# Latent attention, row-maximum and projection matmuls issued ahead of a step's weighted sums, and output weights split one step behind their transfer

## The chip, the cores and the metric

The kernel runs on one core of a Trainium2 chip. The metric is the device time of the whole program in microseconds. The core has a matrix engine (PE, with weight loads shown apart as PEld), a vector engine (DVE), an activation engine (ACT), a general engine (POOL) and an engine that issues transfers (SP). Each takes its instructions strictly in the order in which the program holds them, and waits at the head of that order for what the instruction needs.

## The reference, cut to what matters

One decoder layer on 1024 tokens of width 1024: an adaLN-modulated norm, one input projection, two groups of heads (sparse attention and latent attention), a gate, one output projection. The change lies in the latent attention and in the loading of the output weights:

```python
def mla_block(args):
    qn, qr, tc = args
    s = (jnp.einsum('bqhd,bkhd->bhqk', qn, k_nope)
         + jnp.einsum('bqhd,bkd->bhqk', qr, k_rot)).astype(jnp.float32) * scale
    p = masked_softmax(s, key_idx[None, :] <= tc[:, None])
    return jnp.einsum('bhqk,bkhd->bqhd', p.astype(v.dtype), v)
...
mixed = jnp.concatenate([o_nsa * jax.nn.silu(z_nsa), o_mla * jax.nn.silu(z_mla)], axis=-1)
x = x + gate[:, None, :] * (mixed @ w_out[l])
```

There are 8 latent heads. Products are kept near float32 by splitting each operand in a high and a low part and adding three matmuls.

## The kernel before, in words

The latent attention has 48 tasks, six for each head (heads 0 to 7, task = 6 x head + 0 to 5). A task is two tiles of 128 keys against up to 512 queries; its score tile is 896, 384, 1024, 1024, 896 and 384 columns wide for the six tasks of a head. The stage runs from about 533 us to 684 us. Step i of its loop (lines 1467 to 1482) does four things:

1. `scores_m(i)`: score matmuls into a PSUM tile `ms` (PE, L1301 to L1306); two exponentials of it on ACT, one in float32 (`lat`, L1314) and one in f16 (`mH`, L1315); their difference `mL` on DVE (L1316).
2. `weigh_m` of task i-3 (the flow is `MLA_LAG` = 3 tasks deep): the weighted sums `mo`, L937, 24 matmuls of 65 columns for a task of 1024 columns, 21 for 896, 9 for 384. After a head's half is complete, `merge_m` (L1324, L1325) scales it on DVE.
3. The entries of `plan` for step i. `max_m(h, ts)` computes raw scores of a later head on PE (`mm`, L1256) and takes their masked row maxima on DVE (`junkm`, `peak`, L1260), five turns in five steps; `peak_split` (DVE, `hl`, L1269 to L1272) and `max_rows` (a transposition `mn` on PE, L1276, a copy `mrow` on DVE, L1278, and two small transfers on SP, L1281) put the maxima in the rows of the queries that the scores of that head use. `kq_up` (L1180) projects keys or queries of a pair of heads and splits them on ACT (`kh`, `qh`, L1189) and DVE (`kl`, `ql`, L1190), with 6 or 12 matmuls at steps 13, 14, 25 and 26; `q_rot` and `v_up` do so at steps 5 to 7.
4. From step 27 on, one step of `load_wo`: a transfer of 256 KB of the output weights (`wor`, L1348, two buffers), its high part on ACT (`woh`, L1349) and its low part (`wol`, L1350) on DVE for odd pieces and on POOL for even ones. Eight pieces at steps 27 to 34. At steps 40 and 43 `mix_load` (L1358 to L1361) is called for the output stage: three transfers and a product on POOL.

`ms`, `mm`, `kq`, `vu`, `qr` and `mn` all take one of three PSUM buffers of 1024 columns. PE's order is the order of the program (`manual_schedule`); the other engines' orders are set by the scheduler of the framework, which hoists work that it takes to be ready, so the transfers of `mix_load` stand on SP just behind the first two of `wor`. The space of the `wor` buffers is that of the projection weights, so the first transfer waits for the last matmul of `kq_up` at step 26.

Of the kernel before, what the change touches and what calls it, by code (L numbers as in the profile page):

```python
# [94 lines left out]
def f32(ap):  # L95
    return ap.bitcast(F32)
# [11 lines left out]
def hybrid_block(ctx, tc, x, c, positions, ada_w, ada_b, norm_g, w_in, cmp_pos, cmp_k_w1, cmp_k_w2,  # L108
# [8 lines left out]
    def pool(stack, name, side="left"):  # L117
        return stack.enter_context(tc.tile_pool(name=name, bufs=1, side=side, reuse_waits="tile"))
# [693 lines left out]
    def drain(gen):  # L812
        for _ in gen:
            pass
# [336 lines left out]
    def slot(name):  # L1151
        return ps[0].tile([P, 1024], F32, tag="s", name=name, bufs=3)
# [136 lines left out]
    def scores_m(i):  # L1289
        h, hf, blks = tasks[i]  # L1290
        z = h % NSETS
        kh, kl, qh, ql = khs[z], kls[z], qhs[z], qls[z]
        pS = slot(f"ms{i}")
        spans, off = [], 0
        for j, c0 in blks:
            n = 512 - c0
            qs = slice(hf * 512 + c0, (hf + 1) * 512)
            ks = slice(j * P, (j + 1) * P)
            dst = pS[:, off:off + n]
            diag = j >= 4 * hf  # L1300
            nc.tensor.matmul(dst, kh[:98, ks], qh[:98, qs], start=n > 128, stop=False, skip_group_check=n < 257)  # L1301
            nc.tensor.matmul(dst, kh[:96, ks], ql[:96, qs], start=False, stop=False, skip_group_check=n < 257)  # L1302
            nc.tensor.matmul(dst, kl[:96, ks], qh[:96, qs], start=False, stop=not diag, skip_group_check=n < 257)  # L1303
            if diag and n != 256:
                two = n == 128
                nc.tensor.matmul(pS[:, off - 256 * two:off - 256 * two + 256 * (1 + two)].rearrange("p (b n) -> p b n", n=256)[:, :, :P]  # L1306
                                 if two else dst[:, :P], identr, dmr[:, None, :].to_broadcast([P, 2, P]) if two else dmr,
                                 start=False, stop=True, skip_group_check=two)
            spans.append((j, c0, off, n))
            off += n  # L1310
        Et = e_tile(i)
        ph = hlp.tile([P, 1024], F16, name=f"mH{i}", tag="H", bufs=HB)
        pl = hlp.tile([P, 1024], F16, name=f"mL{i}", tag="L", bufs=HB)
        nc.scalar.activation(Et[:, :off], pS[:, :off], AF.Exp, scale=SC_MLA)  # L1314
        nc.scalar.activation(ph[:, :off], pS[:, :off], AF.Exp, scale=SC_MLA)  # L1315
        nc.vector.tensor_tensor(pl[:, :off], Et[:, :off], ph[:, :off], op=ALU.subtract)  # L1316
        return spans, ph, pl
# [10 lines left out]
    def weigh_m(i, spans, ph, pl):  # L1328
        h, hf, _ = tasks[i]
        for j, c0, off, n in spans:  # L1330
            if j == 0:
                po_of[hf] = o_bank(f"mo{h}_{hf}", hf)
            for q in range(n // P):
                tq = c0 // P + q
                pv(po_of[hf], tq * 65, ph, pl, P, slice(off + q * P, off + (q + 1) * P), mp["v"][:, j, h],
                   j == 0 and q == 0, j == 4 * hf + 3)
        if spans[-1][0] == 4 * hf + 3:
            merge_m(h, hf)
# [4 lines left out]
    def load_wo(pl, hf):  # L1343
        for k in range(KD):
            woh[hf][k] = q_row((k % 4) + 8 * (k // 4)) if hf else pl.tile([P, 512], F32R, name=f"woh{hf}_{k}")
            wol[hf][k] = wol_place[k] if hf else pl.tile([P, 512], F32R, name=f"wol{hf}_{k}")
            wr = pl.tile([P, 512], F32, name="wor", tag="wor", bufs=2)
            nc.sync.dma_start(wr, w_out[k * P:(k + 1) * P, hf * 512:(hf + 1) * 512])  # L1348
            nc.scalar.activation(woh[hf][k], wr, AF.Copy)  # L1349
            (nc.vector if k % 2 else nc.gpsimd).tensor_tensor(wol[hf][k], wr, f32(woh[hf][k]), op=ALU.subtract)  # L1350
            yield

    mixs = {}

    def mix_load(t, pl):
        mix = mixs[t] = pl.tile([P, D], F32, name=f"mix{t}", tag="mix", bufs=2)
        zn = pl.tile([P, 512], F32, name=f"zn{t}", tag="zn", bufs=1)
        nc.sync.dma_start(mix[:, :512], mix_dram[t * P:(t + 1) * P, :])  # L1358
        nc.sync.dma_start(zn, z_dram[t * P:(t + 1) * P, :512])
        nc.sync.dma_start(mix[:, 512:], z_dram[t * P:(t + 1) * P, 512:])  # L1360
        nc.gpsimd.tensor_tensor(mix[:, :512], mix[:, :512], zn, op=ALU.mult)  # L1361
# [24 lines left out]
    def e_tile(i):  # L1386
        if i < LAG:
            return npool.tile([P, 1024], F32, name=f"mE{i}", tag="E", bufs=EB)
        if i < E_MIX:
            return mixm[1][:, 2 * (i % 2):2 * (i % 2) + 2].rearrange("p a n -> p (a n)")  # L1390
        return lat_flat[:, (i % 2) * 1024:(i % 2 + 1) * 1024]
# [59 lines left out]
    plan = {PLAN0[0]: [(kq_up, 1, 0)]}  # L1451
# [13 lines left out]
    with tc.manual_schedule(engines={mybir.EngineType.PE}):  # L1465
        wo_steps = iter(())
        for i in range(LAG, len(tasks)):
            if i in pre:
                for f, *args in pre[i]:
                    f(*args)  # L1470
            flow.append((i, *scores_m(i)))
            if len(flow) > MLA_LAG:
                weigh_m(*flow.pop(0))
            for f, *args in plan.pop(i, ()):
                f(*args)
            if i == MLA_WO:
                mr.close()
                wo0 = pool(att, "wo0", "right")
                wo_steps = load_wo(wo0, 0)
            next(wo_steps, None)  # L1480
            if i in MLA_MIX:
                mix_load(MLA_MIX.index(i), wo0)
        for f in flow:
            weigh_m(*f)
        drain(wo_steps)
# [5 lines left out]
    for n, tiles in enumerate((khs, qhs, kls, qls)):  # L1491
        wol_place += [tiles[1][:, :512], tiles[1][:, 512:]]
    drain(load_wo(op, 1))
    gf = lat_flat[:, 2048:3072]
    nc.sync.dma_start(gf, bass.AP(tensor=final_norm_g.tensor, offset=final_norm_g.offset, ap=[[0, P], [1, D]]))
# [100 lines left out]
```

## Time and profile before

| | us |
|---|---|
| median of 3 runs (lowest, highest) | 787.88 (786.41, 790.76) |
| the profiled execution, whole | 788.64 |
| its span, first to last instruction | 786.9 |
| mean granted clock of PE | 0.97 of full |
| PE busy in the span | 739.3 (94%) |
| DVE busy in the span | 583.6 (74%) |
| ACT busy in the span | 396.3 (50%) |

The profile is of one execution. [...]

### The profile page before, as it was taken

What the parts mean: (1) busy time and instruction counts of PE and PEld (TensorE: products, weight loads), DVE (VectorE), ACT (ScalarE), POOL (GpSimd) and SP (SyncE); (2) the same over time, 40 slices, a digit from 0 to 9 for tenths busy, and PEclk for the clock granted to TensorE, in tenths of its full rate; (3) what the DMA queues carried; (4) which work ended last, traced back from release to release, by engine and by line L of the source; (5) the groups of instructions that cost most, each with busy time, mean ns of one, the idle gap of its engine ahead of it and who ended that gap; (6) DMA issues with size and microseconds to landing.
All of it is one profiled execution on the core that took longest, in us unless ns stands there. A gap on an engine that the chain in (4) does not pass through costs nothing.

```text
span 786.9 us, 17257 instructions
## 1 busy us (share of the span) xinstructions
PE 739.3 (94%) x6464; PEld 653.9 (83%) x6464; DVE 583.6 (74%) x1549; ACT 396.3 (50%) x697; POOL 228.0 (29%) x287
## 2 busy tenths in 40 slices
PE   4999999999999999997899999999988989999996
PEld 3988998989999999995677887777877777888885
DVE  3688745587688788888898889987888878654433
ACT  5354534133122331217899977987556566632212
POOL 3334433154231143504443312110200040154322
PEclk9599999999999999999999999999999979999999
DMA  8961423242531121103311123013010140435431
GB/s 307 262 197 49 127 55 108 61 121 80 162 95 48 44 52 47 36 31 97 93 47 44 43 56 82 22 57 80 10 28 16 52 151 29 151 131 185 144 113 54
DMA packets 60513, 70.18 MB, mean 89 GB/s; under 512 B 5957, under 2 KB 46728, under 8 KB 60430
## 3 DMA queue, kind: packets, MB, share of 16 engines
q1 hardware_dynamic: 55646, 64.62, 27.8%
q10 hardware_dynamic: 4784, 4.47, 1.7%
q8 instruction: 51, 0.84, 0.4%
q14 instruction: 32, 0.26, 0.1%
HBM read 48.33 MB, written 11.53 MB: 76 GB/s over the span
## 4 chain that ended last, share of the span: by engine, by line
PE 76%; DVE 9%; issue 4%; ACT 4%; DMA 4%; POOL 2%; SPq 1%; POOLq 0%; DVEq 0%; ACTq 0%
PE pj L589 24%; PE out L1528 11%; PE o L937 5%; PE pm L841 4%; PE s L994 3%; PE s L995 3%; PE kcT L321 2%; PE mo L937 2%; PE hid L642 2%; PE kq L1180 2%; PE ms L1301 2%; DVE L L1010 2%; PE ms L1302 2%; PE ms L1303 2%; PE mm L1256 2%
## 5 line engine op out<-in xcount | busy, mean ns | idle before, releaser
L589 PE MATMUL pj<-whi,hh 128*128 128x288 f32 (+2 forms) x544 | 161.4, 297 | 0.0
L589 PE MATMUL pj<-wlo,hh 128*128 128x288 f32 (+2 forms) x544 | 158.6, 292 | 0.0
L589 PE MATMUL pj<-whi,hl 128*128 128x288 f32 (+2 forms) x544 | 157.6, 290 | 0.0
L589 PEld LDWEIGHTS pj<-wlo,hh 128*128 128x128 f32 x544 | 102.5, 189 | 1.4
L589 PEld LDWEIGHTS pj<-whi,hh 128*128 128x128 f32 x544 | 102.5, 189 | 0.4
L589 PEld LDWEIGHTS pj<-whi,hl 128*128 128x128 f32 x544 | 102.2, 188 | 0.0
L1010 DVE TENSOR_TENSOR L<-E,H 128x1024 f16<-128x1024 f32 x74 | 92.0, 1243 | 13.1 <-ACT H L1005 11.4
L799 DVE CUSTOM_DVE_ANT_0 junk<-pm,maskw 128x256 bf16<-128x256 f32 (+3 forms) x160 | 77.7, 486 | 16.4 <-PE pm L841 4.4
L1004 ACT ACTIVATE E<-s 128x1024 f32<-128x1024 f32 x74 | 76.4, 1032 | 19.8 <-PE s L995 12.2
L937 PEld LDWEIGHTS <-H 128*128 128x128 f16 x1184 | 57.2, 97 | 30.2 <-issue 17.5
L968 POOL TENSOR_TENSOR mixn<-mixn,tmp 128x256 f32<-128x256 f32 x32 | 44.8, 1400 | 108.7 <-DVE tmp L967 101.9
L1005 ACT ACTIVATE H<-s 128x1024 f16<-128x1024 f32 x74 | 76.2, 1030 | 0.0
L841 PE MATMUL pm<-ka,qall 128*128 128x448 f32 (+5 forms) x208 | 67.2, 323 | 0.2 <-DVE mp L796 0.2
L937 PE MATMUL o<-v,H 128*128 128x65 f16 (+1 forms) x1056 | 60.0, 195 | 4.6 <-DVE mixn L964 4.6
L211 POOL TENSOR_TENSOR wlo<-wraw,whi 128x288 fp32r<-128x288 f32 (+2 forms) x64 | 51.7, 832 | 31.6 <-ACT whi L210 29.3
L994 PE MATMUL s<-qa,ka 128*128 128x512 f32 x132 | 57.9, 439 | 2.9 <-ACT H L1005 2.5
L937 PE MATMUL o<-v,L 128*128 128x65 f16 x528 | 56.7, 193 | 0.0
L937 PEld LDWEIGHTS <-L 128*128 128x128 f16 x592 | 55.7, 100 | 0.0
L708 ACT ACTIVATE zt<-pj 128x288 f32<-128x288 f32 (+1 forms) x32 | 12.2, 384 | 74.3 <-PE pj L589 62.6
L1314 ACT ACTIVATE lat<-ms 128x1024 f32<-128x1024 f32 (+2 forms) x40 | 32.6, 815 | 31.1 <-PE ms L1303 14.9
L1316 DVE TENSOR_TENSOR mL<-lat,mH 128x1024 f16<-128x1024 f32 (+2 forms) x40 | 39.0, 988 | 9.7 <-ACT mH L1315 9.5
L995 PE MATMUL s<-qall,kb_early 128*128 128x512 f32 x108 | 43.4, 401 | 0.0
(384 smaller groups left out, 1892.1 us busy)
## 6 DMA issues: line engine op xcount, KB each, us to landing
ad<-in_ada_w_dram SPq DMA_DIRECT2D x32, 256.0 KB
wraw<-in_w_in_dram SPq DMA_DIRECT2D x20, 288.0 KB
x<-in_x_dram SPq DMA_DIRECT2D x8, 512.0 KB
gw<-in_ada_w_dram SPq DMA_DIRECT2D x32, 128.0 KB
qa<-qall SPq DMA_DIRECT2D x32, 128.0 KB
wor<-in_w_out_dram SPq DMA_DIRECT2D x16, 256.0 KB
xr<-in_x_dram SPq DMA_DIRECT2D x8, 512.0 KB
out_dram<-y SPq DMA_DIRECT2D x7, 512.0 KB
```

The costliest lines, as they stand in the source:

```text
L211: split.tensor_tensor(wlo[:, :width], raw[:, j, :width], f32(whi[:, :width]), op=ALU.subtract)
L589: nc.tensor.matmul(pt[:, :width], a[k][:, ts], b[:, :width], start=(n == 0), stop=(n == 23))
L799: nc.vector.tensor_tensor_reduce(out=junk[:, :w], in0=scores, in1=mask, scale=1.0, scalar=2.0 * NEG, op0=ALU.add, op1=ALU.max, accum_out=dst)
L841: nc.tensor.matmul(bank[:, :total_w], lhs, keys, start=True, stop=True)
L937: nc.tensor.matmul(po[:, c0:c0 + hi - lo], a[:n, qs], v[:, lo:hi], start=start and j == 0, stop=stop and j == 2, skip_group_check=True)
L968: nc.gpsimd.tensor_tensor(mv, mv, tmp, op=ALU.add)
L994: nc.tensor.matmul(dst, a, staged[u], start=True, stop=False)
L995: nc.tensor.matmul(dst, b, qc[u], start=False, stop=mk is None)
L1004: nc.scalar.activation(Et, pS, AF.Exp, scale=SC_NSA)
L1005: nc.scalar.activation(ph, pS, AF.Exp, scale=SC_NSA)
L1010: nc.vector.tensor_tensor(pl, Et, ph, op=ALU.subtract)
L1528: nc.tensor.matmul(po, a[:, kk], b[hf][k][:, cs.start - hf * 512:cs.stop - hf * 512], start=(n == 0), stop=(n == 23))
```

## The change

In a step, the entries of `plan` (row maxima, their transposition, projections) are now issued before the weighted sums of task i-3 instead of after them. In `load_wo` for the first half of the columns (`hf` = 0) the generator stops right after issuing a transfer, and the split of that piece is issued at the beginning of the next step's turn, ahead of the next transfer. The arithmetic is the same.

```diff
@@ load_wo
             wol[hf][k] = wol_place[k] if hf else pl.tile([P, 512], F32R, name=f"wol{hf}_{k}")
             wr = pl.tile([P, 512], F32, name="wor", tag="wor", bufs=2)
             nc.sync.dma_start(wr, w_out[k * P:(k + 1) * P, hf * 512:(hf + 1) * 512])
+            if not hf:
+                yield
             nc.scalar.activation(woh[hf][k], wr, AF.Copy)
             (nc.vector if k % 2 else nc.gpsimd).tensor_tensor(wol[hf][k], wr, f32(woh[hf][k]), op=ALU.subtract)
-            yield
+            if hf:
+                yield
@@ the loop over the tasks
             flow.append((i, *scores_m(i)))
+            for f, *args in plan.pop(i, ()):
+                f(*args)
             if len(flow) > MLA_LAG:
                 weigh_m(*flow.pop(0))
-            for f, *args in plan.pop(i, ()):
-                f(*args)
             if i == MLA_WO:
                 mr.close()
```

On PE, steps 26 to 28. `kq3_1` is the projection of queries for heads 6 and 7, `mm5_3` the last turn of maxima of head 5, `mn5` their transposition, `ms27` and `ms28` the scores of tasks 27 and 28, `mo` the weighted sums (their weight loads and most of their rows are left out). Before:

```order
L1180 MATMUL kq3_1_9648<-cqh1_4990,wnl_4998 128x512 x2
L1256 MATMUL mm5_3_9665<-kh1_8152,qh1_8155 128x512
L1301 MATMUL ms27_9674<-qall2_845,qall0_843 128x512
...
L937 MATMUL mo4_0_9686<-vm16_8541,mH24_9530 128x65
...
L1276 MATMUL mn5_9708<-ident_66,hl2_9669 16x128
L1301 MATMUL ms28_9724<-qall2_845,qall0_843 128x512
...
L937 MATMUL mo4_0_9686<-vm16_8541,mH25_9579 128x65
```

Of the change:

```order
L1180 MATMUL kq3_1_9636<-cqh1_4990,wnl_4998 128x512 x2
L1256 MATMUL mm5_3_9653<-kh1_8152,qh1_8155 128x512
L937 MATMUL mo3_1_9496<-vm16_8541,mH23_9483 128x65
...
L1301 MATMUL ms27_9674<-qall2_845,qall0_843 128x512
...
L1276 MATMUL mn5_9686<-ident_66,hl2_9657 16x128
L937 MATMUL mo4_0_9692<-vm16_8541,mH24_9530 128x65
...
L1301 MATMUL ms28_9722<-qall2_845,qall0_843 128x512
```

The weighted sums of a task (those of `mH24` here) stood ahead of the transposition of the same step and now stand behind it, ahead of the next scores.

On DVE, the same steps: `junkm` and `peak5` are the maxima of head 5, `kl2`, `kl3` and `ql2` low parts of projections, `mcf` and `mixm1` the merge of head 3's second half, `hl2` the split of the maxima, which `mn5` waits for. Before:

```order
L1190 TENSOR_TENSOR kl2_8543<-kq3_0_9605,kh2_8538 64x1024
L1260 ISA junkm_9622,peak5_9469<-mm5_4_9616,lat_837 128x384
L1324 RECIPROCAL mcf_9645<-mo3_1_9488 128x4
L1325 SCALAR_TENSOR_TENSOR mixm1_8528<-mo3_1_9488,vinv_83,mcf_9645 128x4x64
L1316 TENSOR_TENSOR mL26_9632<-lat_837,mH26_9631 128x1024
L1190 TENSOR_TENSOR kl3_8544<-kq3_0_9605,kh3_8539 64x1024
L1260 ISA junkm_9667,peak5_9469<-mm5_3_9665,lat_837 128x512
L1190 TENSOR_TENSOR ql2_8545<-kq3_1_9648,qh2_8540 64x1024
L1272 TENSOR_TENSOR hl2_9669<-nm_9671,hl2_9669 128x8
```

Of the change:

```order
L1190 TENSOR_TENSOR kl2_8543<-kq3_0_9584,kh2_8538 64x1024
L1260 ISA junkm_9601,peak5_9457<-mm5_4_9595,lat_837 128x384
L1190 TENSOR_TENSOR kl3_8544<-kq3_0_9584,kh3_8539 64x1024
L1316 TENSOR_TENSOR mL26_9632<-lat_837,mH26_9631 128x1024
L1260 ISA junkm_9655,peak5_9457<-mm5_3_9653,lat_837 128x512
L1324 RECIPROCAL mcf_9671<-mo3_1_9496 128x4
L1190 TENSOR_TENSOR ql2_8545<-kq3_1_9636,qh2_8540 64x1024
L1325 SCALAR_TENSOR_TENSOR mixm1_8528<-mo3_1_9496,vinv_83,mcf_9671 128x4x64
L1272 TENSOR_TENSOR hl2_9657<-nm_9659,hl2_9657 128x8
```

The merge (`mcf`, `mixm1`) moved from ahead of `mL26` to between the last maxima and `hl2`.

On ACT, steps 27 to 31: `lat` and `mH` are the two exponentials of a task, `woh0_0` to `woh0_4` the high parts of the output weights, `qh3` the second half of the projected queries. Before:

```order
L1349 ACTIVATE woh0_0_9718<-wor_9720 128x512
L1314 ACTIVATE lat_837<-ms27_9674 128x1024
L1315 ACTIVATE mH27_9681<-ms27_9674 128x1024
L1189 ACTIVATE qh3_8542<-kq3_1_9648 64x1024
L1349 ACTIVATE woh0_1_9756<-wor_9758 128x512
...
L1349 ACTIVATE woh0_2_9808<-wor_9810 128x512
L1314 ACTIVATE lat_837<-ms29_9762 128x384
L1315 ACTIVATE mH29_9770<-ms29_9762 128x384
L1349 ACTIVATE woh0_3_9860<-wor_9862 128x512
L1349 ACTIVATE woh0_4_9908<-wor_9910 128x512
L1314 ACTIVATE lat_837<-ms30_9814 128x896
```

Of the change:

```order
L1351 ACTIVATE woh0_0_9718<-wor_9720 128x512
L1314 ACTIVATE lat_837<-ms27_9674 128x1024
L1315 ACTIVATE mH27_9681<-ms27_9674 128x1024
L1351 ACTIVATE woh0_1_9756<-wor_9758 128x512
L1189 ACTIVATE qh3_8542<-kq3_1_9636 64x1024
...
L1351 ACTIVATE woh0_2_9808<-wor_9810 128x512
L1351 ACTIVATE woh0_3_9860<-wor_9862 128x512
L1314 ACTIVATE lat_837<-ms29_9760 128x384
...
L1314 ACTIVATE lat_837<-ms30_9812 128x896
L1315 ACTIVATE mH30_9821<-ms30_9812 128x896
L1351 ACTIVATE woh0_4_9908<-wor_9910 128x512
```

Piece 0 keeps its place; piece 1 moved ahead of `qh3`, piece 3 ahead of the exponentials of task 29, piece 4 behind those of task 30. On SP the third transfer of `wor` moved ahead of the two small transfers of head 5's maxima; the other transfers kept their places. On POOL the order is the same.

## Rows read from the trace of the kernel before

**Rows 1.** The page: busy us (share of the span) and instructions of each engine.

```profile
PE 739.3 (94%) x6464; PEld 653.9 (83%) x6464; DVE 583.6 (74%) x1549; ACT 396.3 (50%) x697; POOL 228.0 (29%) x287
```

**Rows 2.** Windows, steps 15-23 and 27-35: length, busy us by engine, PEclk, DMA share.

```profile
590.72:613.78 23.06, 20.97 (x244) 17.71 (x245) 19.68 (x44) 15.24 (x20) 0.00 (x0) 1.00 0.08 17
626.10:656.13 30.03, 25.77 (x244) 21.70 (x245) 23.42 (x48) 19.66 (x28) 8.45 (x6) 0.83 0.37 124
```

**Rows 3.** Waits of PE in the whole stage: us in total, times, longest us.

```profile
PE ms L1301 <- DVE ql L1190: 2.8, 2, 1.9
PE ms L1301 <- DVE peak L1260: 2.6, 4, 0.9
PE mn L1276 <- DVE hl L1272: 2.3, 5, 0.7
```

**Rows 4.** Waits of ACT in steps 27 to 35.

```profile
ACT woh L1349 <- DMA wor<-in_w_out_dram: 8.5, 5, 3.6
```

**Rows 5.** Timeline of ACT there: start us, us, line, operation [idle before].

```profile
628.81 0.63 ACT L1349 ACTIVATE woh<-wor 128x512 fp32r<-128x512 f32 x1 [1.98 <-DMA wor<-in_w_out_dram]
629.35 1.01 ACT L1314 ACTIVATE lat<-ms 128x1024 f32<-128x1024 f32 x1
...
635.82 0.49 ACT L1314 ACTIVATE lat<-ms 128x384 f32<-128x384 f32 x1 [0.24 <-PE ms L1306]
...
640.28 0.63 ACT L1349 ACTIVATE woh<-wor 128x512 fp32r<-128x512 f32 x1 [3.58 <-DMA wor<-in_w_out_dram]
642.43 0.63 ACT L1349 ACTIVATE woh<-wor 128x512 fp32r<-128x512 f32 x1 [1.52 <-DMA wor<-in_w_out_dram]
```

**Rows 6.** Timeline of SP in that stretch.

```profile
625.80 0.83 SPq L1348 DMA_DIRECT2D wor<-in_w_out_dram  x2
...
636.16 11.40 SPq L1348 DMA_DIRECT2D wor<-in_w_out_dram  x5
```

**Rows 7.** Timeline of POOL in that stretch.

```profile
632.56 1.26 POOL L1361 TENSOR_TENSOR mix<-mix,zn 128x512 f32<-128x512 f32 x1 [1.76 <-DMA zn<-z_dram]
636.45 1.82 POOL L1361 TENSOR_TENSOR mix<-mix,zn 128x512 f32<-128x512 f32 x1 [2.63 <-DMA zn<-z_dram]
638.23 1.59 POOL L1350 TENSOR_TENSOR wol<-wor,woh 128x512 fp32r<-128x512 f32 x1
```

**Rows 8.** A window of 2 us within that stretch, columns as in rows 2.

```profile
640.00:642.00 2.00, 2.00 (x29) 1.91 (x27) 0.72 (x3) 0.63 (x1) 0.00 (x0) 0.50 0.41 131
```

**Rows 9.** Waits of PE behind the stage.

```profile
PE out L1528 <- DVE ml L1515: 0.9, 1, 0.9
```

**Rows 10.** Waits of PE in steps 18 to 23.

```profile
PE ms L1301 <- DVE peak L1260: 0.5, 1, 0.5
PE mn L1276 <- DVE hl L1272: 0.3, 1, 0.3
```

**Rows 11.** The chain that ended last, weighted sums of two widths: start us, us.

```profile
600.81 0.75 PE mo L937 x24
...
605.60 0.31 PE mo L937 x9
```

**Rows 12.** Timeline of PE, steps 26, 28, 29 and 32.

```profile
622.77 0.71 PE L1180 MATMUL kq<-cqh,wnh 128*128 128x512 f32 x2 [0.92 <-DVE mcf L1324]
...
628.95 0.50 PE L1301 MATMUL ms<-qall,qall 98*128 98x512 f32 x1 [0.37 <-DVE mrow L1278]
...
633.93 0.58 PE L1301 MATMUL ms<-qall,qall 98*128 98x256 f32 x1 [1.87 <-DVE ql L1190]
...
645.49 0.50 PE L1301 MATMUL ms<-qh,kh 98*128 98x512 f32 x1
```

**Rows 13.** Timeline of DVE: a merge, a low part, the last split of maxima.

```profile
622.75 0.48 DVE L1325 SCALAR_TENSOR_TENSOR mixm<-mo,vinv,mcf 128x256 f32<-128x256 f32 x1
...
626.96 1.21 DVE L1190 TENSOR_TENSOR ql<-kq,qh 64x1024 fp32r<-64x1024 f32 x1
628.09 0.15 DVE L1272 TENSOR_TENSOR hl<-nm,hl 128x8 fp32r<-128x8 f32 x1
```

## The prediction

> **What bounds the kernel now.** The page comes first: PE is busy for 94% of the span, DVE for 74% [rows 1]. Behind the stage of the latent attention PE waits once, for 0.9 us [rows 9], so what the stage gains goes nearly whole to the end of the program. Then the windows by stretch. Steps 15 to 23 and 27 to 35 hold the same PE work (244 matmuls each, one projection, nine score tasks), and take 23.06 and 30.03 us [rows 2]. The excess of 7.0 us is the price of the output weights' first half. In the quiet stretch PE is idle for 23.06 - 20.97 = 2.1 us. Third, the list of PE's waits over the stage: for low parts of projections 2.8 us, for maxima 2.6, for the split of maxima 2.3 [rows 3]. Most are waits for one of three PSUM buffers.
>
> Where do the 7.0 us go? ACT waits 8.5 us for transfers of weights [rows 4], with exponentials behind it. Its timeline gives the places: 1.98 us ahead of the exponentials of task 27, 3.58 and 1.52 us ahead of those of task 30 [rows 5]. The second pair has a chain behind it. POOL's product of step-40 data waits for its second transfer until 636.45 and takes 1.82 us; `wol` of piece 2 stands behind it on POOL and ends at 639.82 [rows 7]; this frees the buffer for piece 4, which ACT has at 642.43 [rows 5]. So 2.6 us lie between issue and use.
>
> [...] At half clock PE is busy without a break [rows 8], so part of ACT's lateness is hidden under PE's slowness and the other way round.
>
> **The change, part by part.** No operation is added or removed; only orders move. The sum is made against the profiled 788.64 us, which lies 0.8 us above the median of 787.88; I take the difference and apply it to the median.
>
> *Plan entries ahead of the weighted sums.* One block of weighted sums takes 0.31 to 0.75 us [rows 11]. The score tile that needs the buffer of older maxima gets one such block more between that buffer's last matmul and itself. The matmuls of maxima, which need the buffer of the last task's exponentials, lose one.
>
> - Quiet steps 18 to 23 (head 3): waits are 0.5 us for maxima and 0.3 for their split [rows 10]. The first is shorter than the 0.66 block (between the two of rows 11) that now covers it: gone. The second goes too, since DVE gets its maxima that much earlier. Lost cover: at the second turn of maxima two exponentials of 0.9 us stand against a block of 0.3, the other matmuls of 0.5 and scores of 0.8, so 0.3 us of new wait. Net gain 0.5 (bounds 0 and 0.8).
> - Steps 36 to 39 have the same two waits and no second turn behind them: gain 0.8 (0 to 0.8).
> - Steps 3 to 11: PE is without idle time to step 7; the waits of steps 8 to 11 hang on a DVE that has no free time there. Gain 0.4 (0 to 1).
> - Steps 12 to 17, with a projection: this is the bad place. The transposition now stands ahead of the block that hid its wait, and on DVE the merge (0.48, with a small reciprocal ahead of it) moved between the last maxima and their split [rows 13]. Worked for step 27, which has the same order: the high part of the second half of keys is on ACT at 623.7, its low part and one low part of exponentials (1.2 us each, as the one of rows 13) end at 626.2, the maxima at 626.9, reciprocal, low part of queries, small splits and merge at 628.8, the last split at 629.0, against 628.24 before [rows 13]. PE is done with the scores at 627.0 and waits 2.0 us. The next scores start at 629.8 instead of 628.95 [rows 12]. The 0.85 us come back at the scores after those, which had to wait for queries anyway (0.9 of the 2.8 us in rows 3). Gain 0.1 (-0.9 to 0.5).
>
> Sum outside the output weights: 0.5 + 0.8 + 0.4 + 0.1 = 1.8 us.
>
> [...] The row puts the idle time of the quiet stretch at 2.1 us [rows 2], which caps what order alone can win there. [...]
>
> *The split one step behind its transfer.* The text of the program delays each split, but ACT's order says otherwise: piece 0 keeps its place ahead of task 27, piece 1 goes ahead of the second copy of queries, piece 3 ahead of task 29; pieces 4 and 6 go back one task. Worked on the clock of before, step 25 beginning as there:
>
> - The projection of step 26 starts at 622.1 instead of 622.77 [rows 12], since its maxima reach DVE earlier; so the first transfer, which waits for it, goes out at 625.1 instead of 625.80 [rows 6], and all that hangs on SP and POOL moves by 0.7.
> - Piece 0 is on ACT at 628.1 (PE, waiting for the split until 629.0, doesn't notice), task 27's exponentials end at 630.6, piece 1 at 631.2, the copy of queries at 632.2, its low part at 633.8: task 29 starts at 633.85, before 633.93 [rows 12]. No gain to here.
> - Piece 3 is issued at 633.6 instead of 636.16 [rows 6], because its buffer's `wol` now stands early on DVE. It lands by 636.4 and is split by 637.1. Task 29's exponentials, which before started at 635.82 [rows 5], come behind it at 637.1 to 638.0. But before, task 30 had to wait for piece 4 until 643.06; now it follows at 638.0 to 639.7.
> - Piece 4 lands at 641.7 (chain of rows 7, 0.7 earlier) and is split by 642.3. Task 31's exponentials end at 643.2, and task 32, which needs that buffer, starts then: 2.3 us ahead of 645.49 [rows 12].
> - Pieces 5 to 7 cost what they did; the gain at task 36 is 2.5 us at full clock.
>
> If the clock falls again, PE's 10 us of work from 629.8 to the end of task 32 takes more, in slack that is some 4 us; about 1 us of the 2.5 is lost. The waits of 2.0 and 1.75 us are at least as long as the 1.87 of before, so I count it: 1.6. Bounds: -1 (clock low over all of it, transfers as slow as piece 3 of before) and 7.0 (all of the excess).
>
> Sum: 1.8 + 1.6 = 3.4 us, 787.9 - 3.4 = **784.5 us**.
>
> **The rivals.** A measurement of this kernel can tell about 0.5% (3.9 us) from no change.
>
> *The excess goes whole.* If transfers land before their turn on ACT, and with no wait over 1 us the clock stays at 1.00, all of the 7.0 us go, with 1.8 beside: 779. For it: pieces 3 and 4 are issued earlier. Against: piece 0 keeps its place with 2 us to wait.
>
> *The wait only moves.* Piece 1 holds up the queries, piece 3 task 29, the merge the split of maxima; what is won at task 32 is lost again at pieces 6 and 7, which stand together ahead of task 33. Then 0 to 1.5 us, 787. For it: the dates to task 29 come out equal above.
>
> *Slower.* The transposition at the head of PE's queue. PE takes nothing past it, so each head whose split is late idles PE by all of the delay. If that costs 2 us in five heads and two more stretches run at half clock (10 us each at half speed, half of it in slack, 2.5 us lost each), the loss is 10 + 5 - 3.4 = 11.6: 799. It decides from about 1 us of wait per head. Against: outside the two projection steps the split has only small work ahead of it. [...]
>
> **How the numbers follow.** Forecast 784.5 with a range of its own of 781.5 to 787: 0.45. Excess gone whole: 0.2. Wait only moves: 0.26. Slower: 0.09. The range 779.5 to 788.5 reaches to the first rival and past the second, leaving out the third and half of the first. Faster by over 0.5% means below 783.9: the first rival, half of the forecast, 0.43; within 0.5%: 0.48; slower: 0.09.
>
> **What would show it.** Right: steps 36 to 39 without the waits for maxima and split; PE waiting some 2 us for `hl` at steps 15 and 27; ACT's wait for `wor` down from 8.5 to about 4 us, the longest ahead of task 27; task 32 starting 16.5 to 18 us behind task 27's scores (before 19.4, 626.10 to 645.49). Wrong: a clock at 1.00 throughout with PE's waits at 33 us (excess gone), or PE waiting for `hl` over 1 us in heads 4, 6 and 7 (slower).

## The result, and the profile after

The changed kernel is slower: 795.12 us in the median of 16 runs (787.96 to 799.06) against 787.88 (785.25 to 793.11), a ratio of 1.0066 (95% interval [1.0044, 1.0087]). A second series gave 795.72 us and 1.0059 [1.0030, 1.0087]. The forecast was 784.5 us, with a range of 779.5 to 788.5.

The profiled execution took 795.27 us, with a span of 793.5. The page gives busy us by engine. Against [rows 1] PE is busy for 5.1 us more with the same instructions.

```profile
PE 744.4 (94%) x6464; PEld 658.4 (83%) x6464; DVE 585.8 (74%) x1549; ACT 395.5 (50%) x697; POOL 227.4 (29%) x287
```

The windows of the stage come next, by steps (length, then busy us of PE, PEld, DVE, ACT and POOL, granted clock as a share of PE's full speed, DMA share, GB/s). Of before, steps 0 to 11, 18 to 23, 24 to 26, 27 to 35 (that row is in [rows 2]) and 36 to 39, and the sum from the scores of task 0 to those of task 47:

```profile
532.97:578.36 45.39, 43.12 (x404) 35.83 (x405) 38.22 (x66) 27.66 (x34) 6.85 (x7) 1.00 0.16 38
...
599.19:613.78 14.59, 13.76 (x165) 11.83 (x164) 12.61 (x31) 9.01 (x12) 0.00 (x0) 1.00 0.09 21
613.78:626.10 12.32, 11.30 (x103) 9.30 (x101) 10.61 (x22) 6.87 (x9) 0.00 (x0) 1.00 0.08 18
...
656.13:666.28 10.15, 9.31 (x112) 7.74 (x111) 8.86 (x24) 5.51 (x8) 0.00 (x0) 1.00 0.07 25
...
sum 146.24, PE 134.69 PEld 113.02 DVE 117.99 ACT 91.70 POOL 15.30; mean PE 16.84 PEld 14.13 DVE 14.75 ACT 11.46 POOL 1.91
```

The changed kernel, steps 0 to 11, 12 to 14, 15 to 17, 18 to 23, 24 to 26, 27 to 35, 36 to 39, and the same sum:

```profile
530.60:579.77 49.17, 45.17 (x404) 37.29 (x405) 38.69 (x67) 27.43 (x34) 6.33 (x7) 0.95 0.17 41
579.77:592.49 12.72, 12.24 (x105) 10.18 (x102) 8.06 (x17) 7.03 (x9) 0.00 (x0) 0.91 0.01 2
592.49:602.86 10.37, 8.57 (x87) 7.05 (x84) 8.45 (x17) 6.15 (x8) 0.00 (x0) 0.84 0.07 16
602.86:616.68 13.82, 13.71 (x169) 11.80 (x166) 12.13 (x31) 9.05 (x12) 0.00 (x0) 1.00 0.10 21
616.68:628.40 11.72, 11.22 (x107) 9.29 (x103) 9.18 (x20) 7.00 (x9) 0.00 (x0) 1.00 0.06 13
628.40:663.50 35.10, 28.76 (x251) 24.36 (x247) 28.22 (x54) 19.41 (x28) 9.20 (x6) 0.72 0.34 106
663.50:672.83 9.33, 9.33 (x114) 8.05 (x112) 6.78 (x21) 5.09 (x7) 0.00 (x0) 0.97 0.06 22
...
sum 155.15, PE 141.92 PEld 119.41 DVE 119.34 ACT 91.42 POOL 15.53; mean PE 17.74 PEld 14.93 DVE 14.92 ACT 11.43 POOL 1.94
```

The last row is read first. The stage is 155.15 - 146.24 = 8.9 us longer. PE's idle time grew from 146.24 - 134.69 = 11.6 to 155.15 - 141.92 = 13.2 us, by 1.7; its busy time grew by 7.2 with the same matmuls. So one fifth is waiting and four fifths are a slower PE. By place, steps 27 to 35 lose 5.1 us against [rows 2], steps 0 to 11 lose 3.8 and steps 15 to 17 lose 1.9 (23.06 - 14.59 = 8.5 before); steps 18 to 23 and 36 to 39 gain 0.8 each, steps 24 to 26 gain 0.6. Within steps 27 to 35 the first five take 19.0 us instead of 19.4, so the loss lies in steps 32 to 35. First before, then the changed kernel:

```profile
645.49:656.13 10.64, 9.04 (x98) 7.39 (x98) 9.96 (x25) 8.02 (x11) 1.26 (x1) 1.00 0.14 50
```

```profile
647.40:663.50 16.10, 13.21 (x104) 10.94 (x100) 12.49 (x27) 7.93 (x11) 2.10 (x2) 0.70 0.12 35
```

Four windows of the changed kernel laid over the stretches at low clock; before has one in the stage, of 10.2 us, around [rows 8], which begins within the 1.87 us that the scores of task 29 waited [rows 12]. First that one, then the four:

```profile
633.20:643.40 10.20, 9.47 (x72) 8.80 (x73) 7.66 (x13) 4.48 (x8) 4.25 (x4) 0.50 0.37 121
```

```profile
575.10:581.90 6.80, 6.80 (x51) 6.02 (x50) 4.57 (x11) 1.39 (x3) 0.00 (x0) 0.51 0.18 40
595.60:598.90 3.30, 3.15 (x27) 2.80 (x28) 2.73 (x5) 1.58 (x2) 0.00 (x0) 0.52 0.01 3
633.10:643.30 10.20, 8.36 (x56) 7.15 (x55) 9.55 (x12) 5.72 (x9) 5.07 (x4) 0.51 0.45 160
653.60:663.80 10.20, 9.69 (x76) 8.63 (x77) 6.59 (x13) 4.05 (x6) 0.00 (x0) 0.51 0.01 3
```

30.5 us at half clock (0.51 and 0.52) instead of 10.2. PE's waits in the stage (us in total, times, longest):

```profile
PE mn L1276 <- DVE hl L1272: 6.3, 5, 1.8
PE ms L1301 <- DVE ql L1190: 1.8, 1, 1.8
PE ms L1301 <- DVE peak L1260: 1.7, 2, 1.0
PE ms L1301 <- DVE mcf L1324: 1.0, 1, 1.0
PE qr L1225 <- DVE ql L1190: 1.0, 1, 1.0
```

Against [rows 3] the wait of the transposition `mn` grew from 2.3 to 6.3 us. Three of its five waits are over 1 us, two of them and the one for `ql` here (start, us, in brackets the idle time ahead):

```profile
631.64 0.28 PE L1276 MATMUL mn<-ident,hl 128*16 128x128 f32 x1 [1.61 <-DVE hl L1272]
...
637.90 0.58 PE L1301 MATMUL ms<-qall,qall 98*128 98x256 f32 x1 [1.84 <-DVE ql L1190]
...
654.11 0.38 PE L1276 MATMUL mn<-ident,hl 128*16 128x128 f32 x1 [1.85 <-DVE hl L1272]
```

The third window above begins 1.5 us behind the first of these waits and holds the second; the fourth begins within the third wait. The second window begins at the end of a wait of 1.62 us at step 15. Ahead of the first window there is no wait of that size: PE waited 0.76, 0.96 and 0.73 us at steps 8 to 10, and the clock fell 0.65 us behind the end of the last (574.59 and 575.24). DVE's timeline says why the split at step 27 is late:

```profile
629.69 0.18 DVE L1324 RECIPROCAL mcf<-mo 128x4 f32<-128x4 f32 x1
629.79 1.18 DVE L1190 TENSOR_TENSOR ql<-kq,qh 64x1024 fp32r<-64x1024 f32 x1
...
631.04 0.47 DVE L1325 SCALAR_TENSOR_TENSOR mixm<-mo,vinv,mcf 128x256 f32<-128x256 f32 x1
631.43 0.15 DVE L1272 TENSOR_TENSOR hl<-nm,hl 128x8 fp32r<-128x8 f32 x1
```

The maxima are ready at 629.77: the last instruction that writes `peak` (L1260) starts at 629.69 and takes 0.08 us. A low part of queries and the merge stand between them and the last split, which ends 1.8 us later; PE, with the transposition at its head, is idle for 1.61 us and begins the weighted sums behind it at 631.75.

At step 33 it is a low part of exponentials that stands there, and POOL splits piece 6 of the output weights in the same time:

```profile
651.62 1.27 POOL L1352 TENSOR_TENSOR wol<-wor,woh 128x512 fp32r<-128x512 f32 x1 [3.39 <-ACT woh L1351]
```

```profile
651.66 2.31 DVE L1316 TENSOR_TENSOR mL<-lat,mH 128x1024 f16<-128x1024 f32 x1
```

This low part takes 2.31 us, where the twelve of this size that no work of POOL overlapped took 1.20 to 1.23 us. In two runs below (e9 and h1) POOL is done with piece 6 before it starts; there it takes 1.22 us, and the transposition waits 0.75 us instead of 1.85.

### The profile page after: what moved, and what is told of

It is laid out like the page before. It is cut to its first block, busy times and chain, and to the rows that moved or that the text cites. A ratio compares the mean times of both kernels' runs of the same rounds, so it can differ in the third digit from the quotient of the medians.

```text
span 793.5 us, 17264 instructions
## 1 busy us (share of the span) xinstructions
PE 744.4 (94%) x6464; PEld 658.4 (83%) x6464; DVE 585.8 (74%) x1549; ACT 395.5 (50%) x697; POOL 227.4 (29%) x287
## 4 chain that ended last, share of the span: by engine, by line
PE 76%; DVE 10%; ACT 5%; issue 4%; DMA 2%; POOL 1%; SPq 0%; POOLq 0%; DVEq 0%; ACTq 0%
PE pj L589 24%; PE out L1531 11%; PE o L937 5%; PE pm L841 4%; PE s L994 3%; PE s L995 3%; PE mo L937 3%; PE kcT L321 3%; PE ms L1301 2%; PE mm L1256 2%; PE hid L642 2%; PE ms L1302 2%; PE ms L1303 2%; DVE L L1010 2%; PE qr L1225 1%
## 5 line engine op out<-in xcount | busy, mean ns | idle before, releaser
L1316 DVE TENSOR_TENSOR mL<-lat,mH 128x1024 f16<-128x1024 f32 (+2 forms) x40 | 41.6, 1043 | 7.8 <-ACT mH L1315 7.8
L1260 DVE CUSTOM_DVE_ANT_0 junkm<-mm,lat 128x1024 bf16<-128x1024 f32 (+7 forms) x48 | 36.1, 752 | 14.4 <-PE mm L1256 13.9
```

## The clock, run by run

The runs of one kernel differ in mean granted clock (for before 0.961 to 0.980), and their time goes with it. A line for each kernel with one slope for all, over 312 executions, gives 5.3 us for 0.01 of clock (standard error 0.2). This splits each kernel's loss: what it costs at equal clock, and what goes with a lower one. It is a split by a fitted line; a wait that slow matmuls hide, and a clock that falls because of a wait, are not told apart by it. Before: 128 executions, mean 789.96 us at 0.9694; on the four chips that they come from, its mean at equal clock is the same within 0.4 us. Changed kernel: 28 executions, mean 795.34 us at 0.9624. Of the 5.4 us, 0.0070 x 534 = 3.7 go with the clock, 1.6 stand at equal clock.

| run | median us | ratio to before | mean clock | us against before at equal clock (standard error 0.4) |
|---|---|---|---|---|
| change, both series | 795.12; 795.72 | 1.0066; 1.0059 | 0.9624 | +1.6 |
| e1_plan_only | 795.05 | 1.0064 [1.0036, 1.0092] | 0.9636 | +1.6 |
| e2_split_only | 789.46 | 1.0000 [0.9969, 1.0032] | 0.9707 | 0.0 |
| e3_mn_behind | 791.22 | 1.0026 [0.9995, 1.0058] | 0.9709 | +2.3 |
| e4_mn_only | 790.75 | 1.0038 [1.0006, 1.0071] | 0.9688 | +1.4 |
| e5_fill4 | 791.75 | 1.0023 [0.9990, 1.0056] | 0.9718 | +2.1 |
| e6_max_only | 791.94 | 1.0047 [1.0010, 1.0085] | 0.9701 | +3.6 |
| e7_max_only_split | 795.63 | 1.0065 [1.0031, 1.0099] | 0.9693 | +4.1 |
| e8_kq_only | 788.46 | 1.0010 [0.9980, 1.0039] | 0.9738 | +1.6 |
| e9_fill_behind | 792.93 | 1.0036 [1.0013, 1.0060] | 0.9732 | +4.7 |
| h1_from12 | 791.17 | 1.0021 [0.9991, 1.0052] | 0.9692 | +1.4 |
| h2_to11 | 792.51 | 1.0018 [0.9987, 1.0049] | 0.9691 | +2.3 |
| g1_ahead_quiet | 790.44 | 1.0007 [0.9984, 1.0030] | 0.9679 | -0.4 |
| g2_wol2_dve | 787.79 | 0.9968 [0.9944, 0.9991] | 0.9732 | -0.3 |

The mean clock of 12 executions is good to about 0.0012 (0.6 us). The part of the program ahead of the stage, which is the same in all of them, ended between 529.5 and 537.6 us in the profiled executions, so single spans are not compared below, only stretches of the stage.

## The experiments

### The two parts of the change

The plan's entries ahead, with the split as before:

```diff
-            if not hf:
-                yield
             nc.scalar.activation(woh[hf][k], wr, AF.Copy)
 ...
-            if hf:
-                yield
+            yield
```

> The plan's entries (maxima, transposition, projections) ahead of the weighted sums as in the changed kernel, the weights' split right behind its transfer as in the kernel before. Theory A (the transposition at the head of PE's queue waits for DVE's split of maxima, and the clock falls behind such waits): the loss is all here, 794 to 796 us, PE's wait of mn for hl over 5 us in the stage, and the stage from the first to the last task's scores near 155 us (before 146.2). Theory B (the later split of the output weights costs it, by the order on ACT): 786 to 788 us, stage near 146 us. Theory C (both needed: each part alone costs nothing, the waits of the two add up at steps 27 to 35): 787 us, with steps 12 to 15 as long as in the changed kernel but 27 to 35 no longer than 31 us.

The split alone (the two `yield` of the change, the loop as before):

> The order of the plan as in the kernel before, the weights' split one step behind its transfer as in the changed kernel. Theory A: no loss, and up to 1.6 us of the gain that the prediction saw in the split: 786 to 788 us, steps 27 to 35 28.5 to 30 us. Theory B: 794 to 796 us, steps 27 to 35 near 35 us and the quiet steps at 23.1 us. Theory C: 787 us.

Measured: 795.05 and 789.46 us. The windows of steps 27 to 35, first e1, then e2:

```profile
630.09:663.59 33.50, 26.72 (x251) 22.59 (x247) 27.14 (x54) 19.59 (x28) 8.92 (x6) 0.80 0.35 111
```

```profile
624.55:654.56 30.01, 24.64 (x244) 20.58 (x245) 23.33 (x48) 19.50 (x28) 9.00 (x6) 0.89 0.38 124
```

All of the loss comes with the plan's entries, so theories B and C fall. The split alone gives nothing: 30.01 us, as the 30.03 of before, though at a higher clock (0.89 against 0.83), so the gain of 1.6 us is not there either.

Nor does the split alone make the order on ACT that the prediction worked with. In e2 pieces 3 and 4 both stand ahead of task 30's exponentials, as before:

```profile
640.89 0.63 ACT L1351 ACTIVATE woh<-wor 128x512 fp32r<-128x512 f32 x1 [2.80 <-DMA wor<-in_w_out_dram]
641.42 0.90 ACT L1314 ACTIVATE lat<-ms 128x896 f32<-128x896 f32 x1
```

In e1, without the later split, piece 3 (at 641.48) goes ahead of task 29's exponentials (642.02) and piece 4 (646.39) behind task 30's (643.65), as in the changed kernel. So this order came with the plan's entries, and no run has it without them. It does not cost time up to task 32, which starts 17.7 us behind task 27 in e1 (before 19.4).

### The transposition alone, behind and ahead

The lines that replace the loop's:

```diff
+            todo_i = plan.pop(i, ())
+            for f, *args in todo_i:
+                if f is not max_rows:   # e4: the loop of before, only "f is max_rows" ahead
+                    f(*args)
             if len(flow) > MLA_LAG:
                 weigh_m(*flow.pop(0))
+            for f, *args in todo_i:
+                if f is max_rows:
+                    f(*args)
```

> The whole change, but the transposition of maxima alone goes behind the weighted sums as before; the matmuls of maxima and projections stay ahead. Theory A: the loss goes, PE's waits of mn for hl come down to the 2.3 us of before or less, the clock is at 1.00 in steps 12 to 17 and 33 to 35, and the sum of the prediction without its clock term holds: 784 to 787 us. Theory B: nothing changes, 794 to 796 us. Theory D (the matmuls of maxima and the projections ahead do the harm, by the wait of scores for low parts of queries as at step 6, 0.99 us): 791 to 795 us with the waits of ms for ql at 5 us or more.

> The kernel before, with only the transposition of maxima moved ahead of the weighted sums. Theory A: the whole loss or more, since the maxima are not earlier than before and so the split isn't either: 794 to 800 us, mn waiting for hl 6 us or more, clock at half in three or more stretches of the stage. Theories B and D: within 0.3% of the kernel before, 786 to 790 us.

Measured: 791.22 and 790.75 us. e3 lies within theory D's range, but without its sign: the scores wait 2.0 us for low parts of queries, not 5. e4 lies between the theories. PE's waits in the stage of e3:

```profile
PE mn L1276 <- DVE hl L1272: 3.7, 4, 1.2
PE ms L1301 <- DMA qh<-mrow: 2.4, 1, 2.4
...
PE mn L1276 <- DVE mcf L1324: 1.2, 1, 1.2
```

With the transposition behind, its clock is that of before, but at equal clock it is the slower one (+2.3 us). The transposition still waits 4.9 us: the merge and the low part stay ahead of the split on DVE, because DVE's order moved with the maxima. And at step 10, one block later, it makes the scores of task 12 wait 2.4 us for the rows that the small transfers bring. e4 costs 1.4 us at equal clock and waits 5.4 us for `hl`. In the profiled executions steps 32 to 35 take 11.6 us in e3 and 17.6 in e4, before 10.6. So theory A holds as to a loss at that place, not as to its being the whole.

### Maxima alone, projections alone

The same loop with `f is max_m` ahead (e6; e7 has the later split beside it), and with all but `max_m`, `max_rows` and `peak_split` ahead (e8).

> The kernel before, with only the matmuls of the maxima moved ahead of the weighted sums; transposition and projections stay behind, the weights' split as before. Theory A: only the gains of the prediction are left (waits for maxima and split at steps 18 to 23 and 36 to 39, 0.5 and 0.8 us), none of the waits at the head of PE's queue: 784 to 787 us where the kernel before stands at 787.9, steps 18 to 23 at 13.8 us. Theory D (projections ahead do the rest of the harm, e3 against before): the same here, since they are not moved. If the maxima ahead did harm by themselves: 789 to 792 us.

> As e6_max_only, and the weights' split one step behind its transfer. Theory A with the forecast's gain of the split: 783 to 786 us, steps 27 to 35 at 28 to 29 us. If the split gives nothing (e2 against before): as e6_max_only within 0.2%.

> The kernel before, with only the projections (and the copies of rows beside them) ahead of the weighted sums; maxima, their split and the transposition stay behind. Theory D (the projections ahead cost what e3 still lost against the version with nothing moved): step 6 at 8.1 us with PE waiting 1.0 us for a low part of queries, 789 to 792 us. Theory A alone: 787 to 788 us, the wait at step 6 given back within the next steps.

Measured: 791.94, 795.63 and 788.46 us. PE's waits in the stage of e6:

```profile
PE ms L1301 <- DVE mcf L1324: 2.4, 1, 2.4
PE ms L1301 <- DMA qh<-mrow: 2.4, 1, 2.4
```

Without any transposition ahead, at an unchanged clock, this is 3.6 us slower at equal clock. The two waits of 2.4 us are its own: scores wait for a merge that came late on DVE, and for the rows that a transposition one block behind makes late; the changed kernel has 1.0 us of the first and none of the second. e8 has the wait of 1.0 us for a low part of queries at step 6 and 1.6 us of loss at equal clock; its median shows nothing of it, with a mean clock of 0.9738 in its runs. "Only the gains are left" fell. e7 differs from e6 by 0.9 us in the mean (794.10 and 793.24), which is within the noise, so the later split gives nothing there either, and its 783 to 786 us was missed.

### Filling the waits

In the changed kernel, ahead of the transposition of heads 3, 5 and 6 (steps 15, 27, 33), and ahead of the scores of task 29 in the same way:

```diff
         pn = slot(f"mn{h}")
+        for _ in range(6 if h in (3, 5, 6) else 0):
+            nc.tensor.matmul(pn[:, 512:].rearrange("p (b n) -> p b n", n=P), identr,
+                             dmr[:, None, :].to_broadcast([P, 4, P]), start=True, stop=True)
```

e9_fill_behind has the same lines behind the transposition.

> The changed kernel, with idle PE time filled in four places: six products of the identity and the mask (128x512 each, into the unused half of the tile that the transposition gets) ahead of the transposition of heads 3, 5 and 6, and seven ahead of the scores of task 29, which overwrite them. They are work that nobody uses, and fill waits of 1.6 to 1.85 us. Theory A1 (most of the loss is the clock, which falls behind these waits): the stretches at half clock behind steps 15, 29 and 33 go, steps 33 to 35 take 8 us or less (changed kernel 12.9), the mean clock rises from 0.959 to 0.968 or more, 788 to 791 us. Theory A2 (the waits themselves are the loss): nothing is shortened, the fill replaces waits, 794 to 797 us with the same clock.

> Control to e5_fill4: the same six products for heads 3, 5 and 6, but issued behind the transposition, where PE does not wait, and the seven ahead of task 29 as there. Theory A1: the waits stay open, the clock falls as in the changed kernel (mean 0.964 to 0.966), and the products come on top: 795 to 799 us. If the products helped by something else than filling the wait (order of buffers, other engines): 790 to 793 us as e5_fill4.

> The changed kernel once more, unaltered, for a second profiled execution on the chip of the three kernels beside it. Theory A1 (exposed waits lower the clock): half clock behind the waits of steps 15, 27 to 29 and 33 again, 25 us or more of the stage at half clock, mean clock of its runs 0.963 to 0.965, 794 to 796 us. If the falls of the first execution were chance: stretches at other places, 788 to 792 us.

Measured: 791.75, 792.93 and 795.72 us. The windows of e5, steps 15 to 17 and 32 to 35, and two of its waits:

```profile
596.56:605.42 8.86, 8.55 (x94) 6.82 (x90) 8.40 (x17) 6.18 (x8) 0.00 (x0) 1.00 0.08 18
```

```profile
650.89:661.49 10.60, 10.44 (x109) 8.51 (x106) 9.28 (x22) 7.50 (x10) 1.28 (x1) 1.00 0.15 47
```

```profile
PE ms L1297 <- DVE ql L1190: 2.9, 1, 2.9
...
PE mn L1278 <- DVE hl L1272: 1.4, 3, 0.7
```

With 25 products that nobody uses the kernel got faster by 4.5 us in the mean (795.34 to 790.81), the clock rose from 0.9624 to 0.9718, and at equal clock it stands 0.5 us above the changed kernel. That is theory A1 in the mean (788 to 791 foreseen; the median lies just above) and in place: steps 32 to 35 take 10.60 us, as the 10.64 of before, where the changed kernel took 16.10. (Steps 33 to 35 take 8.4 us, 8 or less foreseen.) The seven ahead of task 29 filled nothing: they wait for 2.9 us themselves, since that wait is for the buffer.

One difference between the profiles is not the fill's doing. The three waits at steps 8 to 10 (0.76, 0.96 and 0.73 us), ahead of all the products, are the same within 0.01 us in the two executions of the changed kernel and in e1, e5, e9 and h2, whose order up to there is the same. In the first three the clock then stood at half for 6.8 us, in the other three at full.

The second execution of the changed kernel, steps 15 to 17 and the sum:

```profile
596.20:605.05 8.85, 7.09 (x88) 5.77 (x84) 8.38 (x17) 6.17 (x8) 0.00 (x0) 1.00 0.08 18
...
sum 151.84, PE 138.10 PEld 115.86 DVE 118.26 ACT 91.61 POOL 15.30; mean PE 17.26 PEld 14.48 DVE 14.78 ACT 11.45 POOL 1.91
```

Its waits are the same, its idle time too (151.84 - 138.10 = 13.7 us), but steps 15 to 17 ran at full clock: the same 1.6 us in front once lowered it and once did not. The falls behind steps 10 and 33 came back, and with the latter the loss in steps 32 to 35 (15.7 us). In steps 27 to 31 it had 3.4 us at half clock instead of 10.2. The expectation of 25 us at half clock was missed (20.4 us).

The control e9 was to leave the waits open (steps 15 to 17, and the wait in the whole stage):

```profile
593.38:605.17 11.79, 10.00 (x93) 7.79 (x90) 8.53 (x17) 6.16 (x8) 0.00 (x0) 0.86 0.06 14
```

```profile
PE mn L1276 <- DVE hl L1272: 5.2, 5, 1.6
```

It left two of them open, 1.62 us at step 15 and 1.60 at step 27. Behind each the clock stood at half for 3.4 us, from 596.8 and from 634.4, which agrees with theory A1. The other two had changed: the wait at step 33 was 0.75 us, and the one ahead of task 29 was gone; no fall followed there. The mean clock of its runs stayed up (0.9732), so the expected 0.964 to 0.966 was missed, and the products cost 3.1 us at equal clock over the changed kernel, as work that nothing hides. e9 is thus no clean control: it doesn't show that an open wait is harmless.

With work put into these waits the mean clock of e5 stood at 0.9718 instead of 0.9624, and its time was 4.5 us shorter in the mean, the cost of that work included. Which wait causes which fall is not shown: the wait of 1.6 us at step 15 was followed by half clock in the first execution of the changed kernel and in e9, and by full clock in the second one, in e1 and in h1.

### Which steps

```diff
+            todo_i = plan.pop(i, ())
+            ahead = i >= 12             # h2, without the later split: i < 12; g1 and g2: 16 <= i < 24 or i >= 36
+            for f, *args in todo_i if ahead else ():
+                f(*args)
             if len(flow) > MLA_LAG:
                 weigh_m(*flow.pop(0))
+            for f, *args in () if ahead else todo_i:
+                f(*args)
```

> The changed kernel with the old order in the steps up to 11; from step 12 on the plan's entries stay ahead of the weighted sums, and the weights' split one step behind. If steps 3 to 11 are the forecast's failed term: steps 0 to 12 at 45.4 us (changed kernel 49.2 and 49.5), 790.5 to 792.5 us, ratio to before 1.002, mean clock 0.966. If the transposition at steps 15, 27 and 33 carries the loss: 794 to 796 us, ratio 1.005 or more, mean clock 0.964 or less.

> The kernel before with the new order in steps up to 11 alone. If these steps are the failed term: steps 0 to 12 at 47.3 us or 49.3 where the clock falls behind step 10, the rest as before, 791 to 793 us, ratio 1.003. If the loss is in the later steps: the stage as long as before within 0.5 us, 788 to 790 us.

Measured: 791.17 and 792.51 us. Steps 0 to 11, h1 and then h2:

```profile
536.21:581.54 45.33, 43.08 (x404) 35.81 (x405) 38.23 (x66) 27.66 (x34) 6.86 (x7) 1.00 0.16 38
```

```profile
533.52:580.77 47.25, 43.23 (x404) 35.49 (x405) 37.59 (x65) 27.43 (x34) 6.34 (x7) 1.00 0.15 37
```

Steps 0 to 11 cost 47.25 - 45.39 = 1.9 us of plain waiting in h2: 1.0 us for a low part of queries at step 6, and 1.7 us of scores for maxima instead of 0.6. Undone (h1), they take 45.33. Both times came out as foreseen for a failed term there. Neither half alone lowers the mean clock (0.9692 and 0.9691), both together do. At equal clock the halves cost 1.4 and 2.3 us, together more than the 1.6 of the whole; why stays open.

### Keeping what gained

g1 takes the new order only in steps 16 to 23 and from 36 on, with the split of before. g2 has besides the low part of piece 2 on DVE:

```diff
-            (nc.vector if k % 2 else nc.gpsimd).tensor_tensor(wol[hf][k], wr, f32(woh[hf][k]), op=ALU.subtract)
+            (nc.vector if k % 2 or (k, hf) == (2, 0) else nc.gpsimd).tensor_tensor(wol[hf][k], wr, f32(woh[hf][k]), op=ALU.subtract)
```

> The kernel before, with the plan's entries ahead of the weighted sums in steps 16 to 23 and from 36 on alone, where the traces of the changed kernel show its gains (0.75 us in steps 18 to 23, about 1.0 in 36 to 39); the old order elsewhere, the weights' split as before. Theory A: the gains stay and nothing is lost, the stage at 144.5 us where the clock is as before (146.2 there), 786 to 787 us, ratio 0.998. If gains there come back as waits elsewhere: stage at 146 us, ratio 1.000.

> As g1_ahead_quiet, and the low part of piece 2 of the output weights' first half on DVE instead of POOL, where the prediction saw it stand behind the product of step-40 data (its buffer frees 2.6 us late). If that chain is what task 32 waits for: piece 4 is issued 2 us or more earlier than in g1_ahead_quiet, steps 27 to 35 at 28 to 29 us, 784 to 785.5 us. If DVE, which gets 0.7 us of work more there, or the next transfers take its place: steps 27 to 35 at 30 us or more, no difference to g1_ahead_quiet.

Measured: 790.44 us (1.0007) and 787.79 us (0.9968 [0.9944, 0.9991]). Steps 27 to 35 of g1 and of g2:

```profile
622.03:655.68 33.65, 26.76 (x245) 21.50 (x245) 23.27 (x48) 19.50 (x28) 8.62 (x6) 0.80 0.33 111
```

```profile
624.51:652.21 27.70, 24.49 (x245) 20.50 (x245) 23.24 (x48) 19.19 (x28) 7.44 (x5) 0.88 0.42 134
```

g1 missed its 786 to 787 us, though its trace has the gains in steps 18 to 23 (14.1 us, before 14.6) and 36 to 39 (9.4, before 10.2). g2 is the one of fourteen versions that beats before, by 0.3%; as the best of so many it may owe part of that to chance. At equal clock the two do not differ (789.3 and 789.4 us); g2's lead is its clock, 0.9732 against 0.9679. Its steps 27 to 35 came below the expected 28 us, but not for the reason given. Piece 4 is issued 12.6 us behind task 27's scores, in g1 13.5, so 0.9 us earlier and not 2; ACT's waits for weights were 8.4 us, as in [rows 4]. What moved is the order on ACT: in g2 task 30's exponentials (at 638.32) go ahead of piece 4 (639.94); in g1 they stand behind it (638.92), and PE, which waits 3.1 us for them there, does not wait for them in g2. That this raises the mean clock of the runs is likely, with one trace of each, and not shown.

## Why the prediction was wrong, step by step

**Two steps of the prediction failed, and the price of the clock is in both.** The first is "Pieces 5 to 7 cost what they did": steps 32 to 35 take 16.1 us (15.7 in the second execution, 15.8 in e1) instead of 10.64, a loss of 5 us where none was foreseen. The transposition at step 33 waits 1.85 us, and the clock stands at half for 10.2 us from 653.6 on, within that wait; with that wait filled (e5) the steps take 10.60. The second is the gain in steps 3 to 11, below.

The prediction counted one fall of the clock, at the output weights, where before has its 10.2 us at 0.50, with "some 4 us" of slack and "about 1 us of the 2.5 is lost". Measured, 3.7 us of the 5.4 by which the means differ go with the clock, in falls in other steps too. No run shows the "about 1 us". In before the quiet stretch had 2.1 us of idle time with the clock at 1.00 [rows 2]. These were waits of up to 0.9 us; the change made single waits of 1.6 to 1.85, and at steps 8 to 10 three of 0.73 to 0.96 us, which were followed by half clock in three of six executions; so "with no wait over 1 us the clock stays at 1.00", the condition of the first rival, does not hold there: behind step 10 the trace of after has 6.8 us at 0.51.

**Steps 3 to 11**: foreseen a gain of 0.4 us (0 to 1), measured a loss of 1.9 at full clock (h2), 3.8 with the fall behind step 10. I saw that DVE has no free time there, and did not work out that a projection ahead makes `qr` wait 1.0 us for the low part of queries at step 6, and that scores wait 1.7 us for maxima instead of 0.6. This is the second failed term. ("PE is without idle time to step 7" left out a wait of 0.55 us until 538.01, which changes nothing.)

**Steps 12 to 17**: the wait of 2.0 us at steps 15 and 27 was 1.62 and 1.61, its cause on DVE as worked out; at full clock the steps come out even (20.5 us in h1, and in e5 with its fill; 20.8 before). The profiled execution took 23.1 us, the second one 21.3, both with part of it at half clock.

**Steps 18 to 23 and 36 to 39** were right: 0.8 us (foreseen 0.5) and 0.8 (foreseen 0.8), the waits of [rows 10] gone. PE is idle for 13.82 - 13.71 = 0.1 us in steps 18 to 23, so idle time was the cap there.

**The split one step behind**: foreseen 1.6 us of gain, measured none for the split alone (e2). The order on ACT that the gain was worked from came with the plan's entries (e1). In the changed kernel ACT's wait for weights went from 8.5 to 5.1 us (foreseen 4), and ACT waits for PE instead, for the scores:

```profile
ACT lat L1314 <- PE ms L1306: 8.2, 3, 3.4
ACT woh L1351 <- DMA wor<-in_w_out_dram: 5.1, 3, 2.1
```

Task 32 starts 647.40 - 628.40 = 19.0 us behind task 27 (foreseen 16.5 to 18), 10.2 us of them at half clock; in the second execution it is 17.8 us and in e1 17.7. So the gain up to task 32 was there in two of three executions, and was lost again in steps 32 to 35. The rival "the wait only moves" has that place right and its price wrong. "Slower" has the mechanism right: the transposition at the head of PE's queue, and more stretches at half clock. Its price of 799 us took waits in five heads; three (3, 5 and 6) had them over 1 us, heads 4 and 7 none. I set its chance low because "outside the two projection steps the split has only small work ahead of it"; at step 33 a low part of exponentials stood there, drawn out to 2.31 us while POOL worked, and the wait was 1.85 us.

## What to carry to other kernels

Here PE, busy for 94% of the span, often paid for an exposed wait twice: in the wait, and in what the clock did behind it. In the stage its idle time grew by 1.7 us and its busy time, with the same matmuls, by 7.2; by the fitted line 3.7 of the 5.4 us between the means go with the clock. Cost both for every place where a move puts a waiting instruction at the head, and work out the busiest steps as closely as the ones the change is about. Moving the producer's call ahead moves the order of the other engines too, so look at what comes to stand between the producer's last input and its output, and list the orders of all engines for each half of a change before crediting one half with them. When the runs of one kernel scatter by 1%, set their times against their mean clock before comparing kernels.

## What the runs showed of the hardware

A wait of 1.6 us ahead of the same matmuls (step 15) was followed by half clock in two executions and by full clock in three; three waits of 0.73 to 0.96 us at steps 8 to 10 by half clock in three executions and by full clock in three. The clock stood at half while PE was busy without a break: 6.80 us of 6.80 from 575.10 to 581.90. Useless products of 128x512, six of them (1.6 us) at each of three waits and seven at a fourth place, went with a mean clock higher by 0.009 over 790 us, and a time 4.5 us shorter.

In the profiled execution of the changed kernel the low parts of exponentials of 1024 columns took 1.20 to 1.23 us on DVE in the twelve cases without overlap with POOL's work. In the four with it, three took 1.65, 1.95 and 2.31 us (the last at step 33), and the fourth, from 633.68, took 1.22; the low part of weights that DVE did behind it (`wol`, 634.83), overlapped by POOL's product of step-40 data, took 1.76 us instead of the 0.68 of one at 649.32.
